# Two transformer blocks on one core: eight plain tiles before the weight pairs, token sums held behind weight halves, and the sum of squares moved to VectorE

## The chip, the cores and the metric

The kernel runs on one core of one Trainium2 chip. The metric is device time in microseconds of one execution. The kernel before was run three times: median 2497.32 us, from 2495.75 to 2497.36 us.

## What is computed

`x` is one sequence of 512 tokens with 1024 features, all in float32. A first block has two layers, each a mixer (retention, sparse attention, dilated attention) and an MLP; a second block has two layers, an even mixer and an odd mixer (a gated linear recurrence), each followed by a SwiGLU feed-forward part. Cut to what the change touches:

```python
def hybrid_layer(...):                      # first block, twice
    ...
    x = x + mixed @ w_out
    h = rms_norm(x, mlp_norm_w)
    return x + jnp.square(jax.nn.relu(h @ w_up)) @ w_down      # 1024 -> 4096 -> 1024

def second_block(...):
    for layer in range(DEPTH):
        h = rmsnorm(x, mix_pre_g[layer])
        m = even_mixer(h, ...) if layer % 2 == 0 else odd_mixer(h, ...)
        x = x + rmsnorm(m, mix_post_g[layer])
        h = rmsnorm(x, ffn_pre_g[layer])
        x = x + rmsnorm(swiglu(h, ...), ffn_post_g[layer])     # 1024 -> 2816 -> 1024
    return x
```

## The kernel before, in words

Activations lie feature-major: a tile holds 128 features by 512 tokens, so `x` is eight tiles `x[0]` to `x[7]`. Each float32 product is made of three TensorE products of fp32r halves (`mm3`, L326 to L328): high weight by high activation, high weight by low activation, low weight by high activation. A **plain tile** (`fm_tiles` with one weight tile) is eight such triples with 512 columns, 24 matmuls, and gives 128 output features.

`weights` (L265) loads a weight tile by a DMA on SP's queue into `raw` (four buffers), writes its high half `whi` with ScalarE (L273) and its low half `wlo` with VectorE or GpSimd (L274). `whi` and `wlo` have three buffers each, so the high half of a tile can be written only when TensorE is done with the tile three before it.

A **pair** (`seven`, L415) makes two output tiles at once with seven products of 256 columns in place of eight (84 matmuls). It needs sums of weight quarters (`pair_weights`: four GpSimd operations, L406 to L410, two `sum` buffers, then halves `shi`, `slo` at L399 and L400) and sums of token halves. The latter are made once for each feed-forward part by `token_sums` (L364): for k = 0 to 3 two scaled copies of `x` by ScalarE (L372), four subtractions by VectorE (L376 to L379), a high half by ScalarE (L382) and a low half by VectorE (L383). `seven` is a generator that yields three times, so that other work stands between its products.

`mlp` (L969) makes its 4096 hidden features as 32 tiles: 0 to 2 together, token sums, 3 to 5 one by one, and 6 to 31 in pairs. The first pair, `pairs([6])`, and the pair of tiles 8 and 9 stand right behind the plain tiles; then come the down products of the first 1024 hidden features, and so on. At the end the last three products of the last pair are carried out by `between` inside `fm_tiles` of the first three tiles of the last down group (L343): six of the eight hidden tiles go first, for the three tiles each, then the rest of the pair, then the two hidden tiles that it gives.

`swiglu` (L1375) makes gate 0, up 0 and gate 1 together (L1412), then the token sums (L1413), then up 1, gate 2 and up 2 as plain tiles, then pairs.

`post_pre_norm` (L1109) ends both mixers of the second block and its first feed-forward part. For each of eight tiles VectorE multiplies (L1094) and adds to `x` (L1096), ScalarE writes the high half of the scaled `x` (L319) and VectorE the low half (L320); TensorE waits for each such half with the next three weight tiles. Beside it `sumsq` (L495) sums the squares: ScalarE squares (L504), and the first five additions are GpSimd's (L510, `eng`), the sixth VectorE's. The order on each engine within this chain is set by `after` (L479), an ordering without a semaphore; elsewhere the Tile scheduler sets it from the order of the program and what is ready.

Of the kernel before, what the change touches and what calls it, by code (L numbers as in the profile page):

```python
# [161 lines left out]
class Net:  # L162
# [102 lines left out]
    def weights(self, src, width, low=None):  # L265
        nc = self.nc
        step = width // 2 if self.early else width
        raw = self.early.pop(0) if self.early else self.load(src, width)
        hi = self.wp.tile([128, 1056], R, tag="whi", name=self.name("whi"))
        lo = self.wp.tile([128, 1056], R, tag="wlo", name=self.name("wlo"))  # L270
        for a in range(0, width, step):
            sl = slice(a, a + step)
            nc.scalar.activation(hi[:, sl], raw[:, sl], AF.Copy)  # L273
            (low or nc.gpsimd).tensor_sub(lo[:, sl], raw[:, sl], hi[:, sl].bitcast(F))  # L274
        return hi, lo

# [57 lines left out]
    def fm_tiles(self, ws, acts, n=None, between=None):  # L334


        ps = [self.mm_tile() for _ in ws]
        n = n or len(acts)
        together = max(n - 2, 0)
        order = [(k, i) for k in range(together) for i in range(len(ws))]  # L340
        order += [(k, i) for i in range(len(ws)) for k in range(together, n)]
        for at, (k, i) in enumerate(order):
            if between and at == together * len(ws):  # L343
                between()
            w, off = ws[i]
            sl = slice(off + k * 128, off + (k + 1) * 128)
            self.mm3(ps[i], (w[0][:, sl], w[1][:, sl]), acts[k], k == 0, k == n - 1)
            if i == len(ws) - 1 and k in (1, 4, 7):
                self.tick()
        self.catch_up()  # L350
        return ps
# [9 lines left out]

        return [self.get("act", 2 * S, R).bitcast(F) for _ in range(n)]

    def token_sums(self, x, g, spare):  # L364


        nc, out = self.nc, []
        for k in range(4):
            b = spare[4 + k % 2]
            b1, b2 = b[:, :S], b[:, S:]  # L370
            for i, b in enumerate((b1, b2)):
                nc.scalar.activation(b, x[k + 4 * i], AF.Copy, scale=g(k + 4 * i))  # L372
            (b11, b12), (b21, b22) = [(b[:, :256], b[:, 256:]) for b in (b1, b2)]
            f = spare[k]
            t1, t2, t3, t4 = [f[:, 256 * i:256 * i + 256] for i in range(4)]
            nc.vector.tensor_sub(t1, b12, b11)  # L376
            nc.vector.tensor_sub(t2, b22, t1)
            nc.vector.tensor_sub(t3, b22, b12)
            nc.vector.tensor_sub(t4, b21, t2)  # L379
            t = self.get("tok", 4 * S, R)  # L380
            hi, lo = t[:, :2 * S], t[:, 2 * S:]
            nc.scalar.activation(hi, f, AF.Copy)  # L382
            nc.vector.tensor_sub(lo, f, hi.bitcast(F))  # L383
            out.append((hi, lo))
        return out
# [106 lines left out]
        self.bg = None  # L492


    def sumsq(self, chunks, g=None, acc=None, apart=False, eng=None):  # L495


        nc = self.nc
        acc = self.temp("acc", 1) if acc is None else acc
        accs = [acc]  # L500
        for i, t in enumerate(chunks):
            sq = acc if i == 0 else self.temp()
            if g is None:
                nc.scalar.activation(sq, t, AF.Square)  # L504
            else:
                nc.scalar.activation(sq, t, AF.Square, scale=g(i))
            if apart and i == len(chunks) - 1:
                accs.append(sq)
            elif i:
                (eng if eng and i <= 5 else nc.vector).tensor_add(acc, acc, sq)  # L510
        return accs

    def mean_sq(self, accs, dim, eps=EPS, warm=False, scale=None):
# [455 lines left out]
    def mlp(self, l):  # L969
# [40 lines left out]

        up(range(3))
        tok = self.token_sums(x, lambda c: self.v("mlp_norm", 8 * l + c), spare)
        for j in range(3, 6):
            up([j])
        pairs([6])
        for g in range(3):
            pairs([8 * g + 8])
            down(g, 0)
# [90 lines left out]
    def post_pre_norm(self, m, post, pl, pre, l, scale=None):  # L1109
        xg = []  # L1110

        def then(c):
            xg.append(self.split_scaled(self.x[c], self.v(pre, 8 * l + c), self.normed()))
            return self.last_low

        self.post_norm(m, post, pl, then, scale=scale)
        return (xg,) + self.rstd(self.sumsq(self.x, apart=True, eng=self.nc.gpsimd), 1024)

    def store(self, c):
        self.nc.sync.dma_start(self.out[c * 128:(c + 1) * 128, :], self.x[c])  # L1120
# [254 lines left out]
    def swiglu(self, l):  # L1375
# [9 lines left out]
        def scaled(ps):  # L1385
            t = self.temp()
            nc.vector.tensor_mul(t, ps, rb)
            return t
# [21 lines left out]
                    nc.vector.tensor_add(m[j], m[j], ps)  # L1410

        p = self.fm_tiles([plain("gate", 0), plain("up", 0), plain("gate", 1)], xg)  # L1412
        tok = self.token_sums(self.x, lambda c: self.v("ffn_pre", 8 * l + c), spare)  # L1413
        product(0, scaled(p[0]), p[1])
        product(1, scaled(p[2]), self.fm_tiles([plain("up", 1)], xg)[0])
        product(2, scaled(self.fm_tiles([plain("gate", 2)], xg)[0]), self.fm_tiles([plain("up", 2)], xg)[0])
        for g, (first, n) in enumerate(HIDDEN[1:]):
            parts = np.array_split(range(8), 2 * n)
            for i in range(n):
# [40 lines left out]
```

## Time and profile before

| what | value |
|---|---|
| median of three runs | 2497.32 us (2495.75 to 2497.36) |
| the profiled execution, its own time | 2494.87 us |
| its span, first to last instruction | 2493.1 us |
| TensorE matmul, busy | 2357.5 us, 95% |
| VectorE, busy | 1781.8 us, 71% |
| ScalarE, busy | 1216.0 us, 49% |
| GpSimd, busy | 950.3 us, 38% |
| mean granted TensorE clock | 0.981 |
| mean DMA rate | 87 GB/s |

Times are from one profiled execution. A busy share is of the whole span. Stretches in which the granted clock is 0.5 are those at the lower of TensorE's two levels, 1.2 GHz in place of 2.4 GHz.

### The profile page before, as it was taken

How to read it: one execution, taken by the hardware profiler on the slowest of the kernel's cores; microseconds unless marked ns; L12 is line 12 of the kernel's file. 1: busy time of each engine (PE TensorE's matmuls, PEld its weight loads, DVE VectorE, ACT ScalarE, POOL GpSimd, SP SyncE). 2: the span in 40 equal slices, each digit the busy share in tenths (PEclk: the TensorE clock that was granted, in tenths of full speed). 3: DMA queues.
4: the chain of work that ended last, by engine and by line, in shares of the span. 5: the costliest groups of instructions: out<-in, count | busy, mean ns of one | idle time of the engine just before them, and what ended most of it. 6: DMA issues, size and time to landing. Idle time of an engine off the chain costs nothing.

```text
span 2493.1 us, 35232 instructions
## 1 busy us (share of the span) xinstructions
PE 2357.5 (95%) x13521; PEld 2024.7 (81%) x13521; DVE 1781.8 (71%) x2847; ACT 1216.0 (49%) x1977; POOL 950.3 (38%) x647
## 2 busy tenths in 40 slices
PE   9999989999997999899999899899999989799997
PEld 7787878898786878788888786799997767699996
DVE  6978675665479786764656867777787765777786
ACT  5656653443365575533434464544443554544442
POOL 3465343343045642443431442343330452343330
PEclk9999999999999999999999999899999999899998
DMA  4321222333232112233322221233332222233322
GB/s 164 111 64 45 66 85 93 102 102 96 83 96 91 60 33 85 91 93 102 100 87 90 81 64 43 78 109 102 102 95 76 84 77 83 68 104 102 99 85 71
DMA packets 68457, 215.71 MB, mean 87 GB/s; under 512 B 7616, under 2 KB 11840, under 8 KB 68288
## 3 DMA queue, kind: packets, MB, share of 16 engines
q1 hardware_dynamic: 66672, 207.06, 27.2%
q0 software_dynamic: 1472, 6.29, 0.7%
q8 instruction: 106, 1.74, 0.3%
q14 instruction: 63, 0.52, 0.1%
q10 hardware_dynamic: 144, 0.11, 0.0%
HBM read 211.33 MB, written 2.10 MB: 86 GB/s over the span
## 4 chain that ended last, share of the span: by engine, by line
PE 72%; DVE 16%; issue 5%; ACT 4%; POOL 2%; DMA 0%; SPq 0%; POOLq 0%; ACTq 0%; DVEq 0%
PE mm L326 20%; PE mm L328 20%; PE mm L327 20%; PE st L327 2%; PE st L328 2%; PE st L326 2%; DVE x L1096 1%; PE st L312 1%; DVE score L758 1%; DVE m L757 1%; PE st L313 1%; PE st L653 1%; DVE act L292 1%; DVE m L1293 1%; ACT xg L319 1%
## 5 line engine op out<-in xcount | busy, mean ns | idle before, releaser
L326 PE MATMUL mm<-xg,whi 128*128 128x512 f32 (+1 forms) x1280 | 448.0, 356 | 37.0 <-ACT whi L273 22.1
L326 PE MATMUL mm<-act,whi 128*128 128x512 f32 x1160 | 458.7, 398 | 14.2 <-ACT act L280 8.2
L327 PE MATMUL mm<-act,whi 128*128 128x512 f32 x1160 | 460.9, 398 | 2.3 <-POOL act L281 2.3
L328 PE MATMUL mm<-act,wlo 128*128 128x512 f32 x1160 | 461.0, 398 | 0.0
L328 PE MATMUL mm<-xg,wlo 128*128 128x512 f32 (+1 forms) x1280 | 452.2, 354 | 7.0 <-DVE wlo L400 5.8
L327 PE MATMUL mm<-xg,whi 128*128 128x512 f32 (+1 forms) x1280 | 453.9, 355 | 0.2
L273 ACT ACTIVATE whi<-raw 128x1024 fp32r<-128x1024 f32 (+3 forms) x222 | 226.4, 1024 | 383.0 <-PE mm L327 224.1
L274 POOL TENSOR_TENSOR wlo<-raw,whi 128x1024 fp32r<-128x1024 f32 (+3 forms) x109 | 257.7, 2366 | 291.7 <-ACT whi L273 282.3
L326 PEld LDWEIGHTS mm<-xg,whi 128*128 128x128 f32 x1280 | 243.5, 192 | 81.8 <-ACT whi L273 24.9
L327 PEld LDWEIGHTS mm<-xg,whi 128*128 128x128 f32 x1280 | 244.2, 191 | 39.8 <-DVE xg L320 6.6
L328 PEld LDWEIGHTS mm<-xg,wlo 128*128 128x128 f32 x1280 | 243.6, 190 | 40.3 <-DVE wlo L400 6.6
L326 PEld LDWEIGHTS mm<-act,whi 128*128 128x128 f32 x1160 | 219.9, 190 | 64.1 <-ACT act L280 10.7
L327 PEld LDWEIGHTS mm<-act,whi 128*128 128x128 f32 x1160 | 219.4, 189 | 52.1 <-POOL act L281 3.1
L328 PEld LDWEIGHTS mm<-act,wlo 128*128 128x128 f32 x1160 | 219.1, 189 | 50.0 <-DVE wlo L274 0.3
L400 DVE TENSOR_TENSOR slo<-sum,shi 128x1024 fp32r<-128x1024 f32 x128 | 177.1, 1385 | 103.5 <-ACT shi L399 101.6
L406 POOL TENSOR_TENSOR sum<-raw 128x512 f32<-128x512 f32 x64 | 94.1, 1471 | 410.9 <-DVE slo L400 200.7
L399 ACT ACTIVATE shi<-sum 128x1024 fp32r<-128x1024 f32 x128 | 135.7, 1060 | 172.1 <-POOL sum L407 86.4
L400 DVE TENSOR_TENSOR wlo<-raw,whi 128x1024 fp32r<-128x1024 f32 (+1 forms) x128 | 175.4, 1370 | 26.7 <-ACT whi L399 26.6
L274 DVE TENSOR_TENSOR wlo<-raw,whi 128x1024 fp32r<-128x1024 f32 (+2 forms) x113 | 140.0, 1244 | 59.6 <-ACT whi L273 59.6
L281 POOL TENSOR_TENSOR act<-t,act 128x512 fp32r<-128x512 f32 x64 | 107.4, 1694 | 184.2 <-ACT act L280 177.1
L399 ACT ACTIVATE whi<-raw 128x1024 fp32r<-128x1024 f32 (+1 forms) x128 | 107.8, 842 | 140.6 <-PE mm L327 139.5
L409 POOL TENSOR_TENSOR sum<-raw,raw 128x512 f32<-128x512 f32 x64 | 95.5, 1492 | 143.0 <-DVE slo L400 143.0
(282 smaller groups left out, 5410.3 us busy)
## 6 DMA issues: line engine op xcount, KB each, us to landing
raw<-in_w1up SPq DMA_DIRECT2D x64, 512.0 KB, 3.6
raw<-in_w1down SPq DMA_DIRECT2D x64, 512.0 KB, 3.6
raw<-in_gate SPq DMA_DIRECT2D x44, 512.0 KB, 3.6
raw<-in_up SPq DMA_DIRECT2D x44, 512.0 KB, 3.6
raw<-in_w1fm SPq DMA_DIRECT2D x41, 512.0 KB, 3.6
half<-in_down SPq DMA_DIRECT2D x64, 256.0 KB, 2.7
raw<-in_odin SPq DMA_DIRECT2D x16, 512.0 KB, 3.6
raw<-in_w1out SPq DMA_DIRECT2D x16, 384.0 KB, 3.1
```

Source lines behind the costliest of these rows:

```text
L273: nc.scalar.activation(hi[:, sl], raw[:, sl], AF.Copy)
L274: (low or nc.gpsimd).tensor_sub(lo[:, sl], raw[:, sl], hi[:, sl].bitcast(F))
L281: (low or nc.vector).tensor_sub(lo, t, hi.bitcast(F))
L292: (low or nc.vector).tensor_sub(s[other], t[own], s[own].bitcast(F))
L312: mm(ps, a[:, rows], b[hh][:, cols], start=True, stop=False, skip_group_check=True)
L326: mm(ps, w[0], a[0], start=first, stop=False, skip_group_check=True)
L327: mm(ps, w[0], a[1], start=False, stop=False, skip_group_check=True)
L328: self.last_mm = mm(ps, w[1], a[0], start=False, stop=last, skip_group_check=True)
L399: nc.scalar.activation(hi[:, :width], t, AF.Copy)
L400: nc.vector.tensor_sub(lo[:, :width], t, hi[:, :width].bitcast(F))
L406: nc.gpsimd.tensor_add(s1, a21, a22)
L409: nc.gpsimd.tensor_sub(s3, a11, a21)
```

## The change

There are four parts.

1. `mlp`: hidden tiles 6 and 7 are plain tiles too, and `pairs([6])` is gone. It does so in both layers.
2. `fm_tiles`: `between` runs after two hidden tiles (`2 * len(ws)`) in place of six.
3. `swiglu`: the weights of up 1 and gate 2 are prepared in the program ahead of the token sums, and `token_sums` orders its scaled copies for k = 0 and 1 behind the high half of up 1 and those for k = 2 behind the high half of gate 2. It does so in both layers.
4. `sumsq`: all additions of squares are VectorE's. `eng` was passed in `post_pre_norm` alone, which runs three times.

```diff
@@ weights
-            nc.scalar.activation(hi[:, sl], raw[:, sl], AF.Copy)
+            self.last_high = nc.scalar.activation(hi[:, sl], raw[:, sl], AF.Copy)
@@ fm_tiles
-            if between and at == together * len(ws):
+            if between and at == 2 * len(ws):
                 between()
@@ token_sums
-    def token_sums(self, x, g, spare):
+    def token_sums(self, x, g, spare, highs=()):
...
-                nc.scalar.activation(b, x[k + 4 * i], AF.Copy, scale=g(k + 4 * i))
+                copy = nc.scalar.activation(b, x[k + 4 * i], AF.Copy, scale=g(k + 4 * i))
+                if k < len(highs):
+                    self.after(copy, highs[k])
@@ sumsq
-                (eng if eng and i <= 5 else nc.vector).tensor_add(acc, acc, sq)
+                nc.vector.tensor_add(acc, acc, sq)
@@ mlp
-        for j in range(3, 6):
+        for j in range(3, 8):
             up([j])
-        pairs([6])
@@ post_pre_norm
-        return (xg,) + self.rstd(self.sumsq(self.x, apart=True, eng=self.nc.gpsimd), 1024)
+        return (xg,) + self.rstd(self.sumsq(self.x, apart=True), 1024)
@@ swiglu
-        tok = self.token_sums(self.x, lambda c: self.v("ffn_pre", 8 * l + c), spare)
+        w1 = plain("up", 1)
+        high = self.last_high
+        w2 = plain("gate", 2)
+        tok = self.token_sums(self.x, lambda c: self.v("ffn_pre", 8 * l + c), spare, [high, high, self.last_high])
         product(0, scaled(p[0]), p[1])
-        product(1, scaled(p[2]), self.fm_tiles([plain("up", 1)], xg)[0])
-        product(2, scaled(self.fm_tiles([plain("gate", 2)], xg)[0]), self.fm_tiles([plain("up", 2)], xg)[0])
+        product(1, scaled(p[2]), self.fm_tiles([w1], xg)[0])
+        product(2, scaled(self.fm_tiles([w2], xg)[0]), self.fm_tiles([plain("up", 2)], xg)[0])
```

How instructions move is shown at three places. A row gives the line, the operation, what it writes and reads, and the shape; numbers behind a name are buffers. Lines of the changed kernel lie two or three further down.

**VectorE in the chain at the end of the even mixer**, from the fourth tile of `x` on. Before:

```order
L1096 TENSOR_TENSOR x_84<-x_84,m_13661 128x512
L1094 SCALAR_TENSOR_TENSOR m_13731<-m_13731,vec_sb,av_14177 128x512
L320 SCALAR_TENSOR_TENSOR xg_14227<-x_84,vec_sb,xg_14227 128x512
L1096 TENSOR_TENSOR x_85<-x_85,m_13731 128x512
L1094 SCALAR_TENSOR_TENSOR m_13767<-m_13767,vec_sb,av_14177 128x512
L320 SCALAR_TENSOR_TENSOR xg_14232<-x_85,vec_sb,xg_14232 128x512
L1096 TENSOR_TENSOR x_86<-x_86,m_13767 128x512
L1094 SCALAR_TENSOR_TENSOR m_13835<-m_13835,vec_sb,av_14177 128x512
L320 SCALAR_TENSOR_TENSOR xg_14237<-x_86,vec_sb,xg_14237 128x512
```

Now:

```order
L320 SCALAR_TENSOR_TENSOR xg_14104<-x_83,vec_sb,xg_14104 128x512
L1098 TENSOR_TENSOR x_84<-x_84,m_13543 128x512
L1096 SCALAR_TENSOR_TENSOR m_13613<-m_13613,vec_sb,av_14059 128x512
L513 TENSOR_TENSOR acc_14132<-acc_14132,t_14137 128x512
L320 SCALAR_TENSOR_TENSOR xg_14109<-x_84,vec_sb,xg_14109 128x512
L1098 TENSOR_TENSOR x_85<-x_85,m_13613 128x512
L1096 SCALAR_TENSOR_TENSOR m_13649<-m_13649,vec_sb,av_14059 128x512
L513 TENSOR_TENSOR acc_14132<-acc_14132,t_14140 128x512
L320 SCALAR_TENSOR_TENSOR xg_14114<-x_85,vec_sb,xg_14114 128x512
L1098 TENSOR_TENSOR x_86<-x_86,m_13649 128x512
L1096 SCALAR_TENSOR_TENSOR m_13717<-m_13717,vec_sb,av_14059 128x512
```

The addition of squares (`acc`) stands between each multiplication and the low half; before, it was in GpSimd's queue.

**ScalarE at the start of the first feed-forward part of the second block**, from the last square on; `act` are the scaled copies of `token_sums`, `tok` their sums' halves, `rb` the spread norm factor. Before:

```order
L504 ACTIVATE t_14270<-x_88 128x512
L372 ACTIVATE act_14294<-x_81,vec_sb 128x512
L372 ACTIVATE act_14294<-x_85,vec_sb 128x512
L372 ACTIVATE act_14295<-x_82,vec_sb 128x512
L372 ACTIVATE act_14295<-x_86,vec_sb 128x512
L372 ACTIVATE act_14294<-x_83,vec_sb 128x512
L572 ACTIVATE rb_14285<-av_14389 128x512
L382 ACTIVATE tok_14417<-act_14290 128x1024
L382 ACTIVATE tok_14426<-act_14291 128x1024
L372 ACTIVATE act_14294<-x_87,vec_sb 128x512
L372 ACTIVATE act_14295<-x_84,vec_sb 128x512
L372 ACTIVATE act_14295<-x_88,vec_sb 128x512
```

Now:

```order
L507 ACTIVATE t_14152<-x_88 128x512
L273 ACTIVATE whi_14295<-raw_14293 128x1024
L273 ACTIVATE whi_14301<-raw_14299 128x1024
L373 ACTIVATE act_14176<-x_81,vec_sb 128x512
L575 ACTIVATE rb_14167<-av_14271 128x512
L373 ACTIVATE act_14176<-x_85,vec_sb 128x512
L373 ACTIVATE act_14177<-x_82,vec_sb 128x512
L373 ACTIVATE act_14177<-x_86,vec_sb 128x512
L1383 ACT_TABLE_LOAD
L1383 ACTIVATE t_14341<-t_14341 128x512
L385 ACTIVATE tok_14311<-act_14172 128x1024
L385 ACTIVATE tok_14320<-act_14173 128x1024
```

The high halves of up 1 and gate 2 stand ahead of all copies; before, that of up 1 stood six rows behind the last row shown here. On VectorE the last rows before the low half of up 2 (`wlo_14410`) are now:

```order
L281 TENSOR_TENSOR act_14345<-t_14341,act_14345 128x512
L386 TENSOR_TENSOR tok_14329<-act_14174,tok_14329 128x1024
L386 TENSOR_TENSOR tok_14338<-act_14175,tok_14338 128x1024
L1384 TENSOR_TENSOR t_14348<-t_14348,mm_14350 128x512
L1389 TENSOR_TENSOR t_14405<-mm_14380,rb_14167 128x512
L274 TENSOR_TENSOR wlo_14410<-raw_14407,whi_14409 128x1024
```

The low half of up 2 stands behind all token sums and behind the reading of gate 2's result (`mm_14380`); before, the three low halves of up 1, gate 2 and up 2 stood in one row behind the token sums.

**TensorE in the last down group of the first layer's MLP**, behind the second hidden tile (`act_5331` before, `act_5272` now). Before:

```order
L326 MATMUL mm_5940<-act_5331,whi_5929 128x512
L327 MATMUL mm_5940<-act_5331,whi_5929 128x512
L328 MATMUL mm_5940<-act_5331,wlo_5930 128x512
L326 MATMUL mm_5939<-act_5727,whi_5923 128x512
L327 MATMUL mm_5939<-act_5727,whi_5923 128x512
L328 MATMUL mm_5939<-act_5727,wlo_5924 128x512
```

Now:

```order
L326 MATMUL mm_5881<-act_5272,whi_5870 128x512
L327 MATMUL mm_5881<-act_5272,whi_5870 128x512
L328 MATMUL mm_5881<-act_5272,wlo_5871 128x512
L326 MATMUL st_5757<-xg_3129,shi_5747 128x256
L327 MATMUL st_5757<-xg_3129,shi_5747 128x256
L328 MATMUL st_5757<-xg_3129,slo_5748 128x256
```

The last products of the pair (`st`, with `shi`) follow here; before, 24 more matmuls of the down group came first.

## Rows read from the trace of the kernel before

**Rows 1.** The page's first part: busy us, share of span, instructions.
```profile
PE 2357.5 (95%) x13521; PEld 2024.7 (81%) x13521; DVE 1781.8 (71%) x2847; ACT 1216.0 (49%) x1977; POOL 950.3 (38%) x647
```

**Rows 2.** Waits of PE, whole span: us in total, times, longest us.
```profile
PE mm L326 <- ACT whi L273: 25.1, 7, 10.7
PE mm L326 <- DVE t L446: 12.7, 6, 4.4
PE mm L326 <- ACT xg L319: 12.0, 15, 0.8
...
PE mm L328 <- DVE wlo L400: 5.8, 2, 2.9
```

**Rows 3.** Stretches: us, busy (instructions) of PE, PEld, DVE, ACT, POOL; PEclk; DMA.
```profile
365.50:368.90 3.40, 3.40 (x18) 3.40 (x18) 2.35 (x6) 2.19 (x4) 0.00 (x0) 0.50 0.53 154
635.10:641.90 6.80, 6.09 (x14) 4.79 (x15) 0.00 (x0) 0.00 (x0) 3.97 (x6) 0.50 0.28 80
1567.00:1580.60 13.60, 6.00 (x13) 4.30 (x14) 11.54 (x17) 9.69 (x13) 0.50 (x1) 0.50 0.23 69
1304.00:1312.00 8.00, 6.87 (x30) 5.27 (x30) 1.45 (x3) 2.27 (x4) 4.99 (x6) 1.00 0.21 66
```

**Rows 4.** Timeline, DVE, end of the mixer: start us, us, instruction, idle before.
```profile
1540.73 1.78 DVE L1096 TENSOR_TENSOR x<-x,m 128x512 f32<-128x512 f32 x1
...
1543.30 0.75 DVE L320 SCALAR_TENSOR_TENSOR xg<-x,vec_sb,xg 128x512 fp32r<-128x512 f32 x1
1543.96 1.80 DVE L1096 TENSOR_TENSOR x<-x,m 128x512 f32<-128x512 f32 x1
...
1556.98 0.69 DVE L1096 TENSOR_TENSOR x<-x,m 128x512 f32<-128x512 f32 x1
1557.58 0.69 DVE L510 TENSOR_TENSOR acc<-acc,t 128x512 f32<-128x512 f32 x1
```

**Rows 5.** Timeline, POOL, same stretch.
```profile
1543.92 1.29 POOL L510 TENSOR_TENSOR acc<-acc,t 128x512 f32<-128x512 f32 x1 [1.97 <-ACT t L504]
```

**Rows 6.** Timeline, PE, start of the second block's two feed-forward parts.
```profile
1574.35 0.79 PE L326 MATMUL mm<-xg,whi 128*128 128x512 f32 x1 [10.73 <-ACT whi L273]
...
2141.28 0.79 PE L326 MATMUL mm<-xg,whi 128*128 128x512 f32 x1 [10.65 <-ACT whi L273]
```

**Rows 7.** Timeline, DVE, start of the first of the two.
```profile
1572.18 2.35 DVE L383 TENSOR_TENSOR tok<-act,tok 128x1024 fp32r<-128x1024 f32 x2
...
1575.05 3.49 DVE L274 TENSOR_TENSOR wlo<-raw,whi 128x1024 fp32r<-128x1024 f32 x3
```

**Rows 8.** Timeline, POOL, same stretch.
```profile
1580.10 1.28 POOL L406 TENSOR_TENSOR sum<-raw 128x512 f32<-128x512 f32 x1 [17.88 <-DMA raw<-in_up]
```

**Rows 9.** Timeline, PE, start of the first layer's MLP.
```profile
338.28 0.40 PE L326 MATMUL mm<-xg,whi 128*128 128x512 f32 x1
...
343.66 0.40 PE L328 MATMUL mm<-xg,wlo 128*128 128x512 f32 x1
...
352.00 0.28 PE L327 MATMUL mm<-tok,shi 128*128 128x256 f32 x1
...
353.91 0.28 PE L327 MATMUL st<-tok,shi 128*128 128x256 f32 x1
```

**Rows 10.** Timeline, DVE, same stretch.
```profile
334.56 1.51 DVE L378 TENSOR_TENSOR act<-act 128x256 f32<-128x256 f32 x1
...
338.87 0.41 DVE L379 TENSOR_TENSOR act<-act,act 128x256 f32<-128x256 f32 x1
339.21 0.41 DVE L377 TENSOR_TENSOR act<-act,act 128x256 f32<-128x256 f32 x1
...
355.34 0.41 DVE L440 TENSOR_TENSOR t<-mm,r 128x256 f32<-128x256 f32 x1
```

**Rows 11.** Timeline, PE, end of the first layer's MLP.
```profile
633.43 0.50 PE L326 MATMUL mm<-act,whi 128*128 128x512 f32 x1 [1.49 <-ACT whi L273]
...
635.81 0.79 PE L327 MATMUL mm<-act,whi 128*128 128x512 f32 x1 [1.13 <-POOL act L281]
```

More of the change, by code (lines that the diff above doesn't have):

```diff
@@ L492, in drain, with sumsq @@
         self.bg = None
-    def sumsq(self, chunks, g=None, acc=None, apart=False, eng=None):
+    def sumsq(self, chunks, g=None, acc=None, apart=False):
         nc = self.nc
```

## The prediction, made before the changed kernel ran

> **What bounds the kernel now.** I read the page's shares first: TensorE is busy for 2357.5 us, 95% of the span, and every other engine much less [rows 1]. So what a change can win is idle time of TensorE, time at its lower clock, or matmuls. Next the waits of TensorE by who ended them [rows 2]. Four entries bear on the change. Two waits of 10.7 us, at the start of the two feed-forward parts [rows 6], are nearly all of the 25.1 us for a high weight half (`whi`, L273). The 15 waits of 0.8 us for `xg` are the chain that ends a mixer, five in each of its three places. Two waits of 2.9 us for `wlo` L400 and two of 4.4 us for L446 stand where the two MLPs go over from plain tiles to pairs. Last the granted clock around such waits [rows 3]: 0.50 in three of the stretches shown, 1.00 in the fourth, which is the end of the second layer's MLP. With the matmuls in them: 18 in 3.4 us, 14 in 6.8 us, 13 in 13.6 us.
>
> The pace of matmuls is start to start. From 338.28 to 343.66 there are 23 steps of 512 columns, 0.234 us each; from 352.00 to 353.91 there are 16 steps of 256 columns, 0.119 us each [rows 9]. I make the sum against the profiled execution (2494.87 us, of which 2493.1 us is span); the median is 2.45 us above it, and I add that at the end.
>
> **Squares added by VectorE (three places).** Before, an addition to `x` took 1.78 to 1.80 us while GpSimd added squares for 1.29 us, and 0.69 us without it [rows 4, 5]: VectorE stands until GpSimd's operation is over. So one tile takes 3.23 us of the chain (from 1540.73 to 1543.96). Now VectorE does four operations per tile, start to start as they stand undisturbed: addition 0.60 (1556.98 to 1557.58), multiplication and low half 0.66 each (1543.30 to 1543.96; both have the same form), addition of squares 0.60, which is 2.52 us. ScalarE's high half lies beside it. TensorE needs 9 x 0.234 = 2.1 us for a tile and so stays behind VectorE. Five tiles win 3.23 - 2.52 = 0.71 us, 3.6 us a place, **10.7 us** in all. GpSimd has nothing else to do there.
>
> One can hold against this that VectorE (71% busy) gets 15 x 0.60 = 9 us more work. The Trainium skill, Perfetto Trace Analysis, section Optimizing Scalar/DVE Operations, says that where VectorE is saturated, moving work to ScalarE or even GpSimd may make sense, though the two share a port. By the first half of this rule a tile would be 0.60 us longer, not 0.71 shorter, and the term a loss of 9 us. I take the rows: 1.8 against 0.69 us.
>
> **Start of the feed-forward parts (two).** Before, TensorE waited 10.73 and 10.65 us for up 1's high half [rows 6], which stood behind the token sums on ScalarE. Now that half needs only TensorE's release of gate 0. It is done about when the spread of the norm ends, and its low half (1.16 us each [rows 7]) follows: I take 0.4 us of wait. The order shows what is late next: the low half of up 2, the last of a row on VectorE. TensorE's wait began at 1563.6 (1574.35 less 10.73). From about 1563.2 on, when VectorE is done with the norm factor's parts, that row is two low halves of weights (2.3 us), 16 subtractions at 0.34 (338.87 to 339.21 [rows 10], 5.4 us), four low halves of sums at 1.17 (2.35 for two [rows 7], 4.7 us) and six shorter operations at 0.60 (3.6 us), then 1.16 us itself: done at 1580.4 if GpSimd is still.
>
> It won't be. The pair's sums wait for a load [rows 8] whose buffer up 1's low half sets free: that half, the first of three from 1575.05 [rows 7], ended at 1576.2, and the first sum began at 1580.10. Now it ends near 1564.3, some 12 us sooner, so four sums (1.3 us each) fall from 1568 to 1574, into the token sums. A held subtraction takes 1.51 us against 0.41 [rows 10], 1.1 us more; the one reading PSUM (L440) is not held (0.41). Four sums cost from 0 (all beside operations on PSUM) to 4.4 us; I take 2.8, since five of the row's operations read PSUM. Low half at 1583.2.
>
> TensorE reaches the matmul that needs it at 1563.6 + 0.4 + 50 x 0.234 + some 0.7 us of the pair's first products = 1576.4, and stands for 6.8 us. With the 0.4 that is 7.2 us in place of 10.7: 3.5 us won. The lower clock cost 3 us before (13 matmuls in 6.0 busy us [rows 3], against 3.0 at 0.234); with a shorter wait I put it at 2.2. Per part 4.3 us, **8.6 us** for both.
>
> **Start of the MLPs (two).** A pair is 84 x 0.119 = 10.0 us, two plain tiles 48 x 0.234 = 11.2 us: 1.2 us more work each. The wait of 4.4 us goes: it came from the sums for tiles 8 and 9 following those of 6 and 7 through two `sum` buffers, and now there are 11 us of plain tiles to make them. With it goes one stretch of 3.4 us at 0.50, in which 18 matmuls of 256 columns took 3.4 and not 2.1 us; with the 0.3 us that other shapes add, 1.6 us. The first wait (2.9 us for a low half [rows 2], and a shorter one for the high half) stays: tile 6's halves take the very places in ScalarE's and VectorE's order that the pair's had, behind the token sums. It grows, since tile 8's four sums and the three low halves of hidden tiles now stand in GpSimd's queue beside the subtractions, one operation more than before: between 0 and 2.2 us (two held subtractions), I take 1.4, a little over one. Per layer 4.4 + 1.6 - 1.2 - 1.4 = 3.4, **6.8 us** for both. What hides the token sums' rest, tile 8's weights and the two extra squarings is the 11 us of tiles 6 and 7; without that cover the 4.4 us come back per layer.
>
> **End of the MLPs (two).** The third down tile's high half takes the buffer of the pair's last weights, so TensorE stood 1.49 us for it and 1.13 us for the low half of a late hidden tile [rows 11]. Now the pair ends after two hidden tiles, and seven matmuls (1.6 us) stand ahead of the third tile, 42 (9.8 us) ahead of the last hidden tiles, which are ready some 5 us after the pair ends. Both waits go: 2.6 us each. In the first layer 6.8 us at 0.50 followed, with 14 matmuls in 6.1 us and not 3.3, so 2.8 us; not in the second [rows 3]. What moves with the pair's end (VectorE's, ScalarE's and GpSimd's few operations on its results) comes where these engines have nothing else. **8.0 us**.
>
> **Sum.** 10.7 + 8.6 + 6.8 + 8.0 = 34.1 us: 2494.87 - 34.1 = 2460.8, at the median 2463.2 us. The highs in `weights` and the order on SP cost nothing: no instruction is added, and each load is issued no later than before.
>
> **The rivals.**
>
> *GpSimd does not hold the token sums* (0.20). For it: several subtractions could share a wait, and operations on PSUM are free. Against it: the held subtraction [rows 10]. The parts then win 2 x 2.8, the MLPs 2 x 1.4: 2455 us; if the MLPs' first wait is covered too (2.9 us, and as much as 1.6 at the lower clock, each), 2446 us.
>
> *The waits only move* (0.12). Each new wait is as long as the old, because the low half of up 2 is held by all of ScalarE's copies too, and the lower clock follows. Then the second and third terms are nil: 2479 us.
>
> *The additions were hidden on GpSimd* (0.04). It holds if an addition to `x` was long for another reason than GpSimd; then 10.7 us won become 9 lost, 2483 us. The Trainium skill's rule above would have it so. Against it: only the additions beside a GpSimd operation are long [rows 4, 5].
>
> *Slower: the shared hold spreads over the whole block of token sums* (0.03). Place: VectorE's row ahead of up 2 and ahead of tile 6, four blocks. If GpSimd had an operation ready for each of 16 subtractions and four low halves, a block would grow by 20 x 1.1 = 22 us, where I count 2.8 or 1.4. That is some 20 us a block, 80 in all on top of the forecast: 2543 us. It decides from 9 us a block, eight GpSimd operations more than the four to seven that stand there. The count speaks against it.
>
> *Nothing measurable* (0.03): 0.2%, or 5 us, is what a measurement of this kernel can tell from no change; all terms would have to fail but one.
>
> **How the numbers follow.** The forecast has 0.58, and its own unknowns (0 to 4.4 twice, 0 to 2.2 twice, clock 0 to 3 us at each wait) move it by some 10 us either way. The range, 2445 to 2479, takes in the second rival and most of the first. Faster by over 0.2%: 0.58 + 0.20 + 0.12 + 0.04 = 0.94; within 0.2% 0.03; slower 0.03.
>
> **What would show it.** In the chain: additions to `x` all near 0.69 us, steps of 2.5 us, TensorE's waits for `xg` at 0.1 to 0.3. At the parts' start: no wait of 10 us at up 1, one of 5 to 8 us for up 2's halves, and GpSimd's four sums within the token sums with subtractions of 1.5 us beside them. In the MLPs: a wait of 4 to 6 us at tile 6, none for L446 of 4 us, none of 1.5 us at the last down group. Wrong would be steps still of 3.2 us without GpSimd, or a new wait of over 11 us at up 2.

## The result and the profile after

The changed kernel takes 2459.26 us (median of four runs, 2454.35 to 2461.55) against 2497.24 us for the kernel before beside it (2495.75 to 2497.36): 38.0 us less, ratio 0.9847, 95% interval 0.983 to 0.9864. The prediction was 2463.2 us, range 2445 to 2479. The profiled execution took 2461.55 us with a span of 2459.8 us, 33.3 us less than the span of before.

The first part of the page of the changed kernel, to be held against [rows 1]:

```profile
PE 2355.4 (96%) x13449; PEld 2020.5 (82%) x13449; DVE 1766.9 (72%) x2848; ACT 1211.6 (49%) x1969; POOL 918.2 (37%) x624
```

TensorE's busy time has hardly changed (2355.4 against 2357.5 us), so nearly all of the gain is idle time. Its waits, as in [rows 2]:

```profile
PE mm L326 <- ACT whi L273: 14.7, 6, 4.9
PE st L833 <- DVE t L827: 10.8, 4, 4.5
...
PE mm L328 <- DVE wlo L274: 6.9, 6, 2.7
...
PE mm L326 <- DVE t L449: 3.8, 4, 0.9
...
PE mm L327 <- DVE xg L320: 2.4, 15, 0.2
```

The two waits of 10.7 us, the two of 4.4 us (L446, now L449) and the 15 of 0.8 us are gone. New in size are the waits for plain tiles' halves: 4.8 and 4.9 us for the high half of up 2, and 2.2 us for the high and 2.7 us for the low half of tile 6, twice each. The row for L827 lies in the first block's mixers; the last section comes back to it.

To see where the time went I cut both traces at the matmuls that spread a norm's factor (L564 before, L567 after) and take the length of each stage. The MLPs are cut once more, at the first matmul of the last down group. The last two columns belong to the kernels with one part each that follow below: the same stages in their traces, and the difference of the medians of the whole time.

| stages | forecast | changed kernel's trace | that part alone, its trace | alone, medians |
|---|---|---|---|---|
| three mixer ends (squares) | -10.7 | -3.63, -3.62, -3.66 = -10.9 | -10.9 | -11.2 |
| two feed-forward parts (start) | -8.6 | -4.30, -4.95 = -9.25 | -9.5 | -9.9 |
| two MLPs, start | -6.8 | -3.75, -3.64 = -7.4 | -8.4 | -7.3 |
| two MLPs, end | -8.0 | -5.71, -2.96 = -8.7 | -8.7 | -10.6 |
| sum of the four parts | -34.1 | -36.2 | -37.5 | -39.0 |
| first block's mixers (untouched) | 0 | +6.36, -2.31 | | |

The remaining untouched stages give -1.1 us together. So the profiled execution won 36.2 us where the change acts, and lost some 3 us elsewhere: in a mixer that no part of the change touches. The last section comes back to that. The medians of the whole time have these mixers in them, each of which is some 4 us longer in some executions than in others, so a part's worth is read from its stages.

Timeline of VectorE at the end of the even mixer, as [rows 4] (in brackets, where they stand, are the engine's idle time before the instruction and what ended it):

```profile
1530.86 0.68 DVE L1098 TENSOR_TENSOR x<-x,m 128x512 f32<-128x512 f32 x1
1531.46 0.74 DVE L1096 SCALAR_TENSOR_TENSOR m<-m,vec_sb,av 128x512 f32<-128x512 f32 x1
1532.12 0.68 DVE L513 TENSOR_TENSOR acc<-acc,t 128x512 f32<-128x512 f32 x1
1532.72 0.74 DVE L320 SCALAR_TENSOR_TENSOR xg<-x,vec_sb,xg 128x512 fp32r<-128x512 f32 x1
1533.39 0.68 DVE L1098 TENSOR_TENSOR x<-x,m 128x512 f32<-128x512 f32 x1
```

An addition to `x` takes 0.68 us where it took 1.8, and a step 2.53 us (1530.86 to 1533.39) where it took 3.23, with one operation more in it.

Timeline of the start of the first feed-forward part, TensorE, ScalarE and VectorE, as [rows 6, 7]:

```profile
1548.09 0.50 PE L328 MATMUL mm<-xg,wlo 128*128 128x512 f32 x1 [0.24 <-DVE wlo L274]
1563.90 0.79 PE L326 MATMUL mm<-xg,whi 128*128 128x512 f32 x1 [4.84 <-ACT whi L273]
```

```profile
1560.84 2.06 ACT L385 ACTIVATE tok<-act 128x1024 fp32r<-128x1024 f32 x2 [2.70 <-DVE act L382]
1562.81 1.04 ACT L273 ACTIVATE whi<-raw 128x1024 fp32r<-128x1024 f32 x1
```

```profile
1552.63 0.92 DVE L382 TENSOR_TENSOR act<-act,act 128x256 f32<-128x256 f32 x1
...
1554.07 3.97 DVE L386 TENSOR_TENSOR tok<-act,tok 128x1024 fp32r<-128x1024 f32 x2
1557.96 1.50 DVE L379 TENSOR_TENSOR act<-act 128x256 f32<-128x256 f32 x1
```

Up 1 is ready after 0.24 us. Up 2's high half, the last of the row on ScalarE, ends the new wait; ScalarE itself had stood 2.70 us for a VectorE subtraction. VectorE was held while GpSimd made the pair's four sums (1551.73 to 1559.18): 0.92 in place of 0.41, 3.97 in place of 2.35, 1.50 in place of 0.41, 3.2 us in all.

The same in the first layer's MLP, TensorE at tile 6, then GpSimd and VectorE ahead of it:

```profile
352.07 0.51 PE L326 MATMUL mm<-xg,whi 128*128 128x512 f32 x1 [2.21 <-ACT whi L273]
...
355.50 0.79 PE L328 MATMUL mm<-xg,wlo 128*128 128x512 f32 x1 [2.70 <-DVE wlo L274]
```

```profile
342.32 1.48 POOL L410 TENSOR_TENSOR sum<-sum,raw 128x512 f32<-128x512 f32 x1
343.76 1.47 POOL L412 TENSOR_TENSOR sum<-raw,raw 128x512 f32<-128x512 f32 x1
345.19 1.48 POOL L413 TENSOR_TENSOR sum<-raw,sum 128x512 f32<-128x512 f32 x1
```

```profile
...
341.13 1.51 DVE L380 TENSOR_TENSOR act<-act,act 128x256 f32<-128x256 f32 x1
342.57 1.51 DVE L379 TENSOR_TENSOR act<-act 128x256 f32<-128x256 f32 x1
344.01 1.50 DVE L382 TENSOR_TENSOR act<-act,act 128x256 f32<-128x256 f32 x1
345.44 1.51 DVE L380 TENSOR_TENSOR act<-act,act 128x256 f32<-128x256 f32 x1
346.87 0.41 DVE L381 TENSOR_TENSOR act<-act 128x256 f32<-128x256 f32 x1
```

Each long subtraction ends within 0.3 us of the end of the GpSimd operation beside it; the first one behind the last sum takes 0.41 us. Five are long here. In the kernel before it was four, that of [rows 10] and these three:

```profile
333.54 1.10 DVE L376 TENSOR_TENSOR act<-act 128x256 f32<-128x256 f32 x1
...
336.00 1.51 DVE L377 TENSOR_TENSOR act<-act,act 128x256 f32<-128x256 f32 x1
337.43 1.52 DVE L376 TENSOR_TENSOR act<-act 128x256 f32<-128x256 f32 x1
```

### The profile page after: what moved, and what is told of

It is laid out like the page before. It is cut to its first block, busy times and chain, and to the rows that moved or that the text cites. A ratio compares the mean times of both kernels' runs of the same rounds, so it can differ in the third digit from the quotient of the medians.

```text
span 2459.8 us, 35068 instructions
## 1 busy us (share of the span) xinstructions
PE 2355.4 (96%) x13449; PEld 2020.5 (82%) x13449; DVE 1766.9 (72%) x2848; ACT 1211.6 (49%) x1969; POOL 918.2 (37%) x624
## 4 chain that ended last, share of the span: by engine, by line
PE 74%; DVE 18%; ACT 4%; issue 3%; POOL 1%; DMA 0%; ACTq 0%; DVEq 0%; POOLq 0%
PE mm L328 21%; PE mm L327 21%; PE mm L326 21%; PE st L328 2%; PE st L327 2%; PE st L326 2%; PE st L312 1%; DVE score L761 1%; PE st L313 1%; DVE m L760 1%; DVE wlo L274 1%; DVE act L292 1%; DVE m L1295 1%; PE st L656 1%; DVE tok L386 1%
## 5 line engine op out<-in xcount | busy, mean ns | idle before, releaser
L326 PE MATMUL mm<-xg,whi 128*128 128x512 f32 (+1 forms) x1296 | 456.7, 358 | 15.9 <-ACT whi L273 14.7
L328 PE MATMUL mm<-xg,wlo 128*128 128x512 f32 (+1 forms) x1296 | 462.2, 358 | 7.1 <-DVE wlo L274 6.9
L327 PE MATMUL mm<-xg,whi 128*128 128x512 f32 (+1 forms) x1296 | 464.0, 358 | 2.6 <-DVE xg L320 2.4
L273 ACT ACTIVATE whi<-raw 128x1024 fp32r<-128x1024 f32 (+2 forms) x226 | 230.7, 1024 | 400.5 <-PE mm L327 237.4
L326 PEld LDWEIGHTS mm<-xg,whi 128*128 128x128 f32 x1296 | 248.2, 192 | 57.6 <-ACT whi L273 17.6
L327 PEld LDWEIGHTS mm<-xg,whi 128*128 128x128 f32 x1296 | 248.2, 192 | 46.7 <-DVE xg L320 11.6
L328 PEld LDWEIGHTS mm<-xg,wlo 128*128 128x128 f32 x1296 | 247.5, 191 | 43.8 <-DVE wlo L274 10.9
L403 DVE TENSOR_TENSOR slo<-sum,shi 128x1024 fp32r<-128x1024 f32 x124 | 167.4, 1351 | 83.0 <-ACT shi L402 81.1
L274 DVE TENSOR_TENSOR wlo<-raw,whi 128x1024 fp32r<-128x1024 f32 (+2 forms) x117 | 145.6, 1246 | 59.3 <-ACT whi L273 59.1
L403 DVE TENSOR_TENSOR wlo<-raw,whi 128x1024 fp32r<-128x1024 f32 x124 | 167.9, 1354 | 26.6 <-ACT whi L402 26.6
L402 ACT ACTIVATE whi<-raw 128x1024 fp32r<-128x1024 f32 x124 | 104.4, 842 | 145.8 <-PE mm L327 145.8
L551 POOL TENSOR_TENSOR rstd<-var,mhalf 128x4 f32<-128x4 f32 x14 | 14.9, 1067 | 354.0 <-DVE var L533 249.0
```

What stands on the lines that cost most here:

```text
L273: self.last_high = nc.scalar.activation(hi[:, sl], raw[:, sl], AF.Copy)
L326: mm(ps, w[0], a[0], start=first, stop=False, skip_group_check=True)
L327: mm(ps, w[0], a[1], start=False, stop=False, skip_group_check=True)
L328: self.last_mm = mm(ps, w[1], a[0], start=False, stop=last, skip_group_check=True)
L402: nc.scalar.activation(hi[:, :width], t, AF.Copy)
L403: nc.vector.tensor_sub(lo[:, :width], t, hi[:, :width].bitcast(F))
```

## The experiments

Ratios are to runs of the kernel before on the same chip, whose median was 2496.24 us beside the first four kernels, 2496.43 beside the next four and 2496.09 beside the last three. What is won or lost in microseconds is the difference of the medians, where no trace or stage is named.

### Each part alone

The first four kernels are the kernel before with one part of the diff. The fourth part:

```diff
-                (eng if eng and i <= 5 else nc.vector).tensor_add(acc, acc, sq)
+                nc.vector.tensor_add(acc, acc, sq)
```

> Only the fourth part (all additions of squares on VectorE, three places) on the kernel before. Theory (VectorE stood beside GpSimd's additions): the steps of the chain fall from 3.23 to 2.52 us, five tiles in three places, 10.7 us less: about 2486.5 us, ratio 0.9957. Rival (the additions were hidden on GpSimd and 15 x 0.60 us are added to VectorE): 9 us more, about 2506 us, ratio 1.0036.

Measured: 2485.05 us, ratio 0.9957, interval 0.9945 to 0.997: 11.2 us less. Against forecast and rival (plus 9 us) that settles the term. That rival followed the Trainium skill, Perfetto Trace Analysis, section Optimizing Scalar/DVE Operations, where it says that a saturated VectorE may offload some work even to GpSimd. The Trainium skill warns in the same section that the two share a port, so that moving work between them might not help; this run bears the warning out.

The third part (weights of up 1 and gate 2 ahead of the token sums):

```diff
+        w1 = plain("up", 1)
+        high = self.last_high
+        w2 = plain("gate", 2)
+        tok = self.token_sums(..., spare, [high, high, self.last_high])
...
```

> Only the third part (up 1's and gate 2's weights ahead of the token sums, feed-forward parts) on the kernel before. Theory (up 1's high half stood behind the token sums on ScalarE; the next wait, at up 2, is shorter): the changed kernel's trace gave 9.2 us for the two places, so 9 us less, about 2488 us, ratio 0.9964, with a wait of about 4.9 us at up 2's high half in place of 10.7 at up 1's. Rival (the waits only move): no change, within 2 us of 2497, waits at up 2 of 9 us or more.

Measured: 2486.33 us, ratio 0.9965 (0.9953 to 0.9977): 9.9 us less. TensorE's waits at up 2 in its trace, first and second layer:

```profile
1580.44 0.80 PE L326 MATMUL mm<-xg,whi 128*128 128x512 f32 x1 [4.82 <-ACT whi L273]
...
2141.84 0.80 PE L326 MATMUL mm<-xg,whi 128*128 128x512 f32 x1 [5.49 <-ACT whi L273]
```

The wait moved by one tile and halved; it did not only move.

The first part (tiles 6 and 7 plain):

```diff
-        for j in range(3, 6):
+        for j in range(3, 8):
             up([j])
-        pairs([6])
```

> Only the first part (hidden tiles 6 and 7 plain, no first pair ahead of them) on the kernel before. Theory (the wait of 4.4 us for L446 and one stretch at 0.50 go, 1.2 us of matmuls and 1.4 us of a longer first wait come): 6.8 us less for both layers, about 2490.5 us, ratio 0.9973. Rival (the cover of two plain tiles is not enough, so the wait for the pair's sums comes back behind tile 7): no gain, 2497 to 2500 us.

Measured: 2488.98 us, ratio 0.9972 (0.9963 to 0.9981): 7.3 us less; the two MLPs are 3.9 and 4.6 us shorter in its trace, 8.4 us of it ahead of the last down group. The wait for the pair's sums did not come back.

The second part (the last pair ends after two hidden tiles):

```diff
-            if between and at == together * len(ws):
+            if between and at == 2 * len(ws):
```

> Only the second part (the last pair's last products after two hidden tiles in place of six) on the kernel before. Theory (waits of 1.49 and 1.13 us go in both layers, and in the first layer the 6.8 us at 0.50 behind them, 2.8 us): 8.0 us less, about 2489.2 us, ratio 0.9968. Rival (the clock stretch came from something else and stays): 5.2 us less, about 2492 us, ratio 0.9979, with a stretch at 0.50 still near 635 us.

Measured: 2485.66 us, ratio 0.9962 (0.9949 to 0.9974): 10.6 us less by the medians, about 6.5 to 12.7 by the interval, so neither 8.0 nor, strictly, 5.2 plus some clock is excluded by the time alone. The traces tell more. No wait of over 0.5 us is left at either end. The ends of the two MLPs, from the last down group on, are 5.8 and 2.95 us shorter than in the trace of before, 8.7 us together, near the 8.0 of the forecast. The rest of the median's 10.6 us is not this edit's: in its trace the second mixer of the first block, which it does not touch, is 3.8 us shorter.

The stretch at the lower clock, which the forecast gave to the first layer alone because [rows 3] show it there, belongs to neither layer: in the trace of the third part alone, which leaves both MLP ends as they were, it stands in the second layer. The same view as [rows 3], for that kernel:

```profile
633.00:641.00 8.00, 5.38 (x34) 4.31 (x33) 3.46 (x5) 3.25 (x5) 2.63 (x2) 1.00 0.12 22
1304.70:1308.00 3.30, 3.25 (x8) 2.58 (x9) 0.00 (x0) 0.00 (x0) 3.11 (x5) 0.50 0.45 149
```

From the last down group on, the two layers take 71.4 and 70.5 us in the trace of before and 68.5 and 72.0 us here. Four traces have the ends as they were, and in each exactly one layer has the stretch: the first in those of before and of the first part alone, the second in those of the third and of the fourth part alone. It costs 2.8 us in the first layer and 1.5 us in the second. So this part is worth 7.3 to 8.7 us, whichever layer has it: both ends together take 140.5 to 141.9 us in these four, and 133.2 us in all nine traces of kernels with the second part.

The four medians add up to 39.0 us, the change to 38.0; in the stages it is 37.5 and 36.2. So the parts hardly disturb each other.

### What holds the token sums

The changed kernel, with the first pair's GpSimd sums held until VectorE's last token-sum subtraction:

```diff
-            nc.vector.tensor_sub(t4, b21, t2)
+            self.hold = nc.vector.tensor_sub(t4, b21, t2)
...
-        nc.gpsimd.tensor_add(s1, a21, a22)
+        first = nc.gpsimd.tensor_add(s1, a21, a22)
+        if self.hold is not None:
+            self.tc.add_manual_dep(first.ins, self.hold.ins.name, mybir.DependencyInfo(
+                mybir.DependencyClass.Sync, mybir.DependencyReason.DATA), reason="apart")
...
```

> The changed kernel, with the first pair's four GpSimd sums of each MLP and each feed-forward part held until VectorE's last token-sum subtraction. Theory (GpSimd's sums hold VectorE's token sums): the subtractions of 1.36 to 1.51 us fall to 0.41; in the MLPs 5 x 1.1 us less, so the waits of 2.2 and 2.7 us at tile 6 and most of the 2.6 us that the lower clock costs behind them go, 5 to 7.5 us each; in the feed-forward parts 3.2 us less of the wait of 4.85 us and up to 2 us of clock. Sum 16 to 25 us, so 2434 to 2443 us against 2459.3. Rival (GpSimd does not hold them, the subtractions are long for another reason): the waits stay, 2457 to 2462 us. Second rival (the sums, now later, become the new wait at the pair): 2459 us or more, with a wait for a sum's half (shi or slo) at the pair.

Measured: 2448.61 us, ratio 0.9808 (0.9795 to 0.9822): 10.7 us less than the changed kernel by the medians, where 16 to 25 were expected. Timeline of VectorE in the first MLP, then of GpSimd:

```profile
335.26 1.35 DVE L381 TENSOR_TENSOR act<-act 128x256 f32<-128x256 f32 x1
336.54 0.41 DVE L380 TENSOR_TENSOR act<-act,act 128x256 f32<-128x256 f32 x1
...
```

```profile
344.26 4.49 POOL L409 TENSOR_TENSOR sum<-raw 128x512 f32<-128x512 f32 x1 [7.92 <-DVE act L382]
```

Fifteen of the sixteen subtractions take 0.41 or 0.42 us; the one that stands beside another GpSimd operation, a hidden tile's low half, still takes 1.35. The waits of 2.2 and 2.7 us are gone (0.77 us is left, and a new one of 1.3 us stands in the pair) and so is the stretch at 0.50; the MLPs are 5.3 and 5.6 us shorter than in the changed kernel. That is the first theory, and the forecast's rival "GpSimd does not hold the token sums" falls. In the feed-forward parts both theories came true in turn. TensorE there:

```profile
1544.27 0.51 PE L326 MATMUL mm<-xg,whi 128*128 128x512 f32 x1 [1.77 <-ACT whi L273]
...
1550.73 0.58 PE L326 MATMUL mm<-tok,shi 128*128 128x256 f32 x1 [5.01 <-ACT shi L402]
```

The wait at up 2 fell from 4.84 to 1.77 us, by the 3.1 us that the hold had cost, and the later sums became a new wait of 5.01 us at the pair. So the parts, which were to gain 3.2 us or more each, are 0.1 us shorter and 1.1 us longer.

### Taking the last halves out of the row

The changed kernel, with up 2's weights too ahead of the token sums:

```diff
-        w2 = plain("gate", 2)
+        w2, w3 = plain("gate", 2), plain("up", 2)
+        last = self.last_high
-        tok = self.token_sums(..., [high, high, self.last_high])
+        tok = self.token_sums(..., [high, last, last, last])
...
```

> The changed kernel, with up 2's weights too prepared ahead of the token sums in the feed-forward parts, and the scaled copies for k = 1 to 3 ordered behind its high half. Theory (the remaining wait of 4.85 us is up 2's halves behind the token sums on ScalarE and VectorE): the wait goes in both layers, and with it the stretches at 0.50 (10.2 and 6.8 us, of which 8.5 and 6.7 us lie behind the wait: 4.2 and 3.3 us), 17 us less: about 2442 us. Rival (the wait moves on to the pair, whose token sums are then the late ones, since they start later): half of it or less, 2451 us or more, with a wait for tok or for the pair's halves.

Measured: 2452.30 us, ratio 0.9831 (0.9816 to 0.9845): 7 us less than the changed kernel by the medians, 2.2 and 1.8 us in the two stages (most of the rest lies in the untouched mixers). My figure of 17 us was wrong; the rival's (half or less) was right, though by another wait than it named. TensorE at up 2:

```profile
1556.30 0.80 PE L326 MATMUL mm<-xg,whi 128*128 128x512 f32 x1 [2.72 <-DVE t L1384]
```

L1384 is the first hidden tile's product. It reads up 0 from PSUM and so frees the buffer that up 2 needs; it now stands behind the token sums on VectorE.

The same for the MLPs: the token sums placed behind hidden tiles 3 and 4, tiles 6 and 7 prepared ahead of them (`made(j)` prepares tile j's weights).

```diff
         up(range(3))
+        up([3])
+        up([4])
+        w5, w6 = made(5), made(6)
+        high = self.last_high
+        w7 = made(7)
         tok = self.token_sums(..., [None, high, high, self.last_high])
...
```

> The changed kernel, with the MLP's token sums placed in the program behind hidden tiles 3 and 4, tile 6's and 7's weights prepared ahead of them, and the scaled copies ordered behind those high halves. Theory (the waits of 2.2 and 2.7 us at tile 6 are its halves behind the token sums): both go in both layers, 9.8 us, and the stretch at 0.50 with them, 2.6 us each: 15 us less, about 2444 us. Rival (the token sums come too late for the first pair): a wait of 5 us or more for tok or its halves in the pair, no gain or a loss, 2457 to 2465 us.

Measured: 2456.31 us, ratio 0.9839 (0.9825 to 0.9852). The stages gained 0.9 and 1.6 us, not 15: near the rival's time, though by another wait than it named. Both waits at tile 6 went, and the first pair got one:

```profile
365.55 0.58 PE L328 MATMUL mm<-xg,wlo 128*128 128x256 f32 x1 [4.37 <-DVE wlo L403]
```

It is neither `tok` nor a sum's half but the low half of the pair's own weights, which now stands behind the later token sums on VectorE.

Both edits together:

> Both of the two before together. Theory (the four waits are apart from each other): the gains add up, about 32 us less than the changed kernel, 2427 us. Rival (the waits move on to the pairs): 2445 us or more.

Measured: 2452.51 us, ratio 0.9819 (0.9805 to 0.9832). No 32 us, but the rival's 2445 or more: each wait of TensorE that went was followed by another of 2.7 to 4.3 us.

### The best of them

The sums held apart in the MLPs alone, up 2 ahead in the feed-forward parts:

> The changed kernel, with the first pair's sums held behind the token sums in the MLPs alone, and up 2's weights ahead of the token sums in the feed-forward parts. Theory (the stages are apart from each other): the stages as they were in the two single experiments, 5.3 and 5.6 us less in the MLPs and 2.2 and 1.8 us less in the feed-forward parts than in the changed kernel's trace, 15 us in all: about 2444 us. Rival (part of those gains was chance of the clock): 2449 us or more.

Measured: 2446.38 us, ratio 0.9797 (0.9783 to 0.981). The MLPs are 5.2 and 5.6 us shorter than in the changed kernel, the feed-forward parts 2.1 and 0.8: 13.6 us in the stages, where 15 were expected. The median lies between the theory's 2444 and the rival's 2449 us. All of its executions (2442.13 to 2447.57 us) lie below all of the changed kernel's.

The same with `product(0, ...)` ahead of `token_sums`:

> The kernel of the run before it, with the first hidden tile's product placed in the program ahead of the token sums. Theory (the 2.7 us that TensorE still waits at up 2 are for the PSUM buffer of up 0, which VectorE's product lets go only behind the token sums): the wait goes in both feed-forward parts, and most of the 3.4 us at 0.50 behind it: 6 to 8 us less, about 2437 us. Rival (the token sums, now some 3 us later, become the wait at the pair): no gain, 2442 us or more, with a wait for tok or for the pair's halves of 2 us or more.

Measured: 2446.23 us, ratio 0.9796 (0.9783 to 0.981), no gain. The wait for L1384 went, and the token sums, later now, became the wait in the pair, as the rival had it, but in pieces of 0.85, 1.62 and 0.65 us:

```profile
1554.77 0.39 PE L327 MATMUL mm<-tok,shi 128*128 128x256 f32 x1 [0.85 <-DVE tok L386]
1556.89 0.38 PE L326 MATMUL mm<-tok,shi 128*128 128x256 f32 x1 [1.62 <-ACT tok L385]
...
```

In both orders TensorE ends up waiting for the same row of VectorE: what was moved up in it made something else late.

The changed kernel a second time:

> The changed kernel as it is, a second time. Theory (the two mixers of the first block differ by 4 to 6 us from one execution to the next, although no part of the change touches them: 193.9 to 200.3 us and 193.7 to 200.3 us in the traces so far): the first mixer is another length than 200.3 us, or the second another than 196.4 us, by over 1 us, while the chains, the MLPs and the feed-forward parts stay within 1 us where no stretch at 0.50 comes or goes. Rival (these lengths belong to the program): all stages within 0.5 us of the first trace.

Measured: 2456.65 us (2453.41 to 2459.39). The mixers were 195.07 and 199.97 us long, where the first trace had 200.26 and 196.37. The chains, MLPs and feed-forward parts agree within 0.4 us. The theory held. The two medians of the changed kernel differ by 2.6 us, so differences of that size between medians are not told apart from these mixers.

## Why the prediction was right, and where its steps were off

**Squares: right in mechanism and size.** 10.7 forecast, 10.9 in the trace, 11.2 alone. Additions to `x` at 0.68 us and steps of 2.53 us are what was named as the sign.

**Start of the feed-forward parts: right in sum (8.6 forecast, 9.25 in the trace), by two errors that nearly cancel.** The step "the low half of up 2 is what is late" failed: the high half on ScalarE was. TensorE did not stand for the low half at all, since it filled that time with six of the pair's matmuls, so the wait was 5.1 us in place of 7.2. What drove it was as forecast: VectorE's row, held 3.2 us (2.8 forecast) by four sums from 1551.73. The clock's term went the other way: I took 2.2 us with the shorter wait in place of 3.0, but the stretch at 0.50 behind it was still 10.2 us long:

```profile
1562.20:1572.40 10.20, 8.29 (x21) 6.15 (x22) 9.43 (x11) 6.05 (x8) 1.55 (x1) 0.50 0.33 100
```

Its 21 matmuls, 15 of 512 columns and 6 of 256, took 8.29 us and would take 4.2 at 0.234 and 0.119: 4.1 us lost, and 3.4 us in the second layer, more than the 3.0 of before. A wait of half the length cost no less clock. So some 5.6 us of wait a part were won where 3.5 were forecast, and 0.4 to 1.1 us of clock were lost where 0.8 was to be won.

**Start of the MLPs: right, in the hold as in the sum (6.8 forecast; 7.4 in the changed kernel's trace, 8.4 in that of the part alone).** The wait of 4.4 us went, and tile 6's waits summed to 4.9 us, within the 4 to 6 that were named. Before, TensorE stood there for 0.7 and 2.9 us, so the first wait grew by 1.3 us (1.4 forecast), and five subtractions were held in place of four, the one operation more that was counted. What the forecast did not price is the whole of the hold, of which the change adds only that last piece: taking the sums away was worth 5.3 and 5.6 us in the two layers, clock included. The clock's part was not as I put it: not one of two stretches of 3.4 us went, but both, and one of 6.8 us came.

**End of the MLPs: right in waits and size (8.0 forecast; 8.7 in both traces).** Both waits went in both layers (5.2 us forecast; the ends are 2.9 us shorter a layer where no stretch at 0.50 goes with the waits). The 2.8 us of clock were given to the first layer, which showed them in one execution; the traces put them now at the first, now at the second, where they are 1.5 us. That the trace of before had the dearer of the two is luck of 1.3 us.

**The rivals.** "The waits only move" was refuted for the change, and then came true in large part for three of the edits that tried to go further. "GpSimd does not hold the token sums" and "hidden on GpSimd" were refuted by direct runs. The shared hold did not spread over the whole block: 3.2 and about 5 us per block, far from the 9 us from which that rival decided.

## What to carry to other kernels

Look at pairs of engines, not at busy shares: VectorE at 71% took over work from GpSimd at 38% and the kernel got faster, since a short operation on the critical engine (0.68 us) took 1.8 us beside a GpSimd operation of 1.29. Where a wait is removed on an in-order engine, write down what stands next in that row before pricing the gain: here the successor was half as long as the first wait, and for the last halves a wait of 4.8 us was followed by one of 2.7, and 4.9 us by 4.4. Read a term that hangs on the lower clock from more than one execution, since the stretch moves from place to place. And where stages that the change does not touch vary by more than a part is worth, read the part from its own stages and not from the whole time.

## What the runs showed of the hardware that was not expected

**The hold goes both ways.** With the sums moved out of the subtractions, a GpSimd sum of 128x512 took 4.49 us beside VectorE's low halves; the shortest in these traces take 1.25. VectorE in that stretch:

```profile
344.10 1.21 DVE L386 TENSOR_TENSOR tok<-act,tok 128x1024 fp32r<-128x1024 f32 x1
345.24 1.21 DVE L274 TENSOR_TENSOR wlo<-raw,whi 128x1024 fp32r<-128x1024 f32 x1
346.37 1.21 DVE L386 TENSOR_TENSOR tok<-act,tok 128x1024 fp32r<-128x1024 f32 x1
```

The Trainium skill, SBUF — State Buffer, section Who interferes with whom, says that a VectorE operation with two inputs in SBUF contends with a GpSimd operation that reads SBUF, and that the order of issue decides who blocks whom. The trace agrees: long VectorE operations beside GpSimd above, and here the sum, which began 0.16 us behind the first low half and ended 1.17 us behind the third. That it stood for three in a row, and not for one, is what these rows add.

**It also goes with how much one program varies.** The first mixer of the changed kernel was 200.3 us long in one execution and 195.1 in another. The timelines of VectorE and GpSimd in the longer one:

```profile
138.22 2.23 DVE L818 TENSOR_SCALAR mu<-mu 128x8 f32<-128x8 f32 x1
...
144.57 2.82 DVE L827 TENSOR_TENSOR t<-t,rs 128x512 f32<-128x512 f32 x1 [1.36 <-POOL rs L826]
```

```profile
138.03 2.39 POOL L274 TENSOR_TENSOR wlo<-raw,whi 128x1024 fp32r<-128x1024 f32 x1 [1.05 <-issue]
...
144.50 2.34 POOL L274 TENSOR_TENSOR wlo<-raw,whi 128x1024 fp32r<-128x1024 f32 x1
```

And in the other, VectorE, GpSimd:

```profile
139.04 0.17 DVE L818 TENSOR_SCALAR mu<-mu 128x8 f32<-128x8 f32 x1
...
143.40 0.69 DVE L827 TENSOR_TENSOR t<-t,rs 128x512 f32<-128x512 f32 x1 [1.26 <-POOL rs L826]
```

```profile
139.06 2.40 POOL L274 TENSOR_TENSOR wlo<-raw,whi 128x1024 fp32r<-128x1024 f32 x1 [1.48 <-issue]
...
145.47 2.40 POOL L274 TENSOR_TENSOR wlo<-raw,whi 128x1024 fp32r<-128x1024 f32 x1 [2.10 <-ACT whi L273]
```

In the first, GpSimd's weight half began 0.2 us ahead of L818, and an operation on 128x8 values took 2.23 us; the next one began 0.07 us ahead of L827, which took 2.82. In the second, each VectorE operation came first (by 0.02 and by 2.1 us) and took 0.17 and 0.69. TensorE's wait for L827 was 4.54 us in the one and 0.22 in the other:

```profile
147.44 1.11 PE L833 MATMUL st<-const_sb,t 128*128 128x128 f32 x4 [4.54 <-DVE t L827]
```

```profile
144.15 0.65 PE L833 MATMUL st<-const_sb,t 128*128 128x128 f32 x4 [0.22 <-DVE t L827]
```

Which of the two begins first is a matter of a fraction of a microsecond at L818. The other traces show the same two cases: no edit here touches the two mixers of the first block, and there are 13 traces, that of before included. In 11 of these 26 mixers L818 takes 2.2 to 2.3 us, the wait for L827 is 4.5 to 4.6 us and the mixer 198.5 to 200.3 us long; in the other 15 it is 0.17 us, the wait 0.2 to 0.3 us, and 14 of them are 193.7 to 196.6 us long (one is 199.5, by other waits). What shifts it was not tried. But the shorter of the two executions had a stretch at 0.50 just ahead, which the longer had not:

```profile
129.60:133.00 3.40, 2.70 (x12) 2.71 (x13) 3.40 (x9) 0.42 (x1) 0.82 (x2) 0.50 0.46 154
```

```profile
129.60:133.00 3.40, 2.84 (x22) 2.60 (x23) 3.40 (x10) 0.87 (x2) 0.73 (x1) 1.00 0.52 154
```

So it is in all 26: where such a stretch begins 100 to 107 us into the mixer, L818 is short, and in the 11 others none begins there. It begins 8 to 11 us ahead of L818, so it may well be the cause, but no run moved it on purpose: that step is argued, not shown.
